# Swapped-query loads of the first four latent-attention units, issued from ScalarE's DMA queue

## The chip, the cores and the metric

The kernel runs on one core of a Trainium2 chip. The metric is the time of one execution on the device, in microseconds (us). The engines have short names in the rows of the profile: PE is TensorE (matmuls; PEld is its weight loads), DVE is VectorE, ACT is ScalarE, POOL is GpSimd, SP is SyncE. Each works through its own list of instructions in order. A data transfer (DMA) is an instruction too: an engine issues it, and it then runs beside the engines. "SPq" in a row is SyncE issuing DMAs.

## The reference, cut to what matters

Two layers of a decoder trunk, sequence length 1024, width 1024, everything in float32. Each layer projects its input, runs four token mixers (latent attention with a rotary key, stick-breaking attention, forgetting attention, memory attention), gates and merges them, projects the merge and normalises. The change touches the latent attention (MLA):

```python
q = (_rms_norm(c_q, q_norm) @ w_qb).reshape(b, s, 4, 64 + 32)
q_nope, q_pe = q[..., :64], q[..., 64:]
q_pe = _rope(q_pe, cos[:, :, None, :], sin[:, :, None, :])
kv = (_rms_norm(c_kv, kv_norm) @ w_kvb).reshape(b, s, 4, 64 + 64)
k_nope, v_mla = kv[..., :64], kv[..., 64:]
k_pe = jnp.broadcast_to(_rope(k_rope[:, :, None, :], ...), (b, s, 4, 32))
y_mla = _causal_softmax_attention(concat([q_nope, q_pe], -1), concat([k_nope, k_pe], -1), v_mla)
...
merged = sum over the four mixers n of merge_g[n] * ((branch[n] * silu(gate_z[n])) @ w_branch[n])
x = layer_norm(alpha * x + merged @ w_out)
```

## The kernel before

TensorE multiplies in a reduced float32 format, so each value is split into a high and a low part, and a product is made of passes over such parts (L257 to L259 for the projections). For the attention the two parts of a head's query lie above each other in one operand: 64 rows high, 64 rows low. `stack_pair` writes these operands from a projection, `opA` for one head and `opB` for the next: the high parts by ACT (L310), the low parts by DVE (L314). Each holds 512 queries, a "half" of the sequence.

A unit of attention is one head with 256 queries (`qg` is 0 to 3; half = `qg // 2`), and `run` goes through the units in a list. A unit's scores are made per 128 queries in pieces of up to 512 keys, each piece by three matmuls into one tile `sc`: L385 (query operand by keys), L386 (the same slice of the query operand with its high and low rows exchanged, by the same keys), and L388 (rotary part `qpe` by `kpe`). DVE then takes the masked scores' maximum (L443), ACT the exponential (L135), POOL scales (L455), TensorE transposes (L474), and the values follow (L504).

The exchanged slice is `s2` (tile name `s` in the rows), and `swapped` makes it: it takes one of three buffers and copies the two 64-row halves crosswise with two DMAs of 64 KB, L365 and L366. `Unit.prep` calls it, and `run` calls `prep` one unit ahead. A scheduler then orders each engine's instructions from the order in which they are written, so that a DMA stands in its engine's list at about the place where its operand is ready.

The latent attention comes last in a layer. Ahead of it a chain of steps makes its operands: `mla_qpe(half)` projects the rotary queries, rotates them on DVE (L1059 to L1063), splits them (`CAST qrs`, L1065, on ACT for the high part; L1066 on POOL for the low part), stores both parts with four DMAs to a scratch array `qr_d` in device memory (L1069) and loads them back in another layout as four `qpe` tiles (L1074). `mla_q(half)` projects the queries and makes `opA` and `opB`. The order is `mla_qpe(1)`, `mla_q(1)`, `mla_qpe(0)`, `mla_q(0)`. The first two units of the list use half 1, the third and the fourth half 0. Between these steps, and then between the pieces of the units, stands work of `merge`: its matmuls `pg` and `pb`, `tanh` on ACT (`mg`, L135), an accumulation on DVE (`acc`, L1122), and loads of the other mixers' results (`y`, L1086, four at a time, split later at L158 and L159).

All of these DMAs are issued by SyncE, in order. Each raises one of eight counters (`DMAHW0` to `DMAHW7`), which are given out in turn, and a DMA that is given a counter waits until the DMA that had the counter before it has landed; it does so on the engine that issues it, in order.

Of the kernel before, what the change touches and what calls it, by code (L numbers as in the profile page):

```python
# [66 lines left out]
def decoder_trunk(ctx: ExitStack, tc: tile.TileContext, x, x_t, mem_t, positions, w_a, w_s, mla_q_norm, mla_w_qb,  # L67
                  mla_kv_norm, mla_w_kvb, fox_forget_bias, w_out,
                  ln_gain, ln_bias, out, dump=None):
    nc = tc.nc  # L70
    act, dve, pool, pe = nc.scalar, nc.vector, nc.gpsimd, nc.tensor
# [15 lines left out]
    def nm(s):  # L87
        uid[0] += 1
        return f"{s}_{uid[0]}"
# [33 lines left out]
    def f(ap):  # L123
        return ap.bitcast(F32)
# [139 lines left out]
    class Stream:  # L264


        def __init__(self):
            self.next = 0
            self.blocks = []
# [89 lines left out]
        yield  # L359


    def swapped(q, head, qg):
        s2 = tp.tile([P, 256], F32R, tag="s2", name=nm("s2"), bufs=3)
        src = q[head][qg // 2][:, (qg % 2) * 256:(qg % 2) * 256 + 256]
        nc.sync.dma_start(f(s2[0:64, :]), f(src[64:128, :]))  # L365
        nc.sync.dma_start(f(s2[64:128, :]), f(src[0:64, :]))  # L366
        return s2

    class Unit:


        def __init__(self, op, head, qg, kind, aux=None):
            self.op, self.head, self.qg, self.kind, self.aux = op, head, qg, kind, aux
            self.p = []

        def prep(self):
            self.s2 = swapped(self.op["q"], self.head, self.qg)
            if self.kind == "fox":
                self.aux()

# [140 lines left out]
    def drain(g):  # L521
        for _ in g:
            pass

    def steps(g, n):
        for _ in range(n):
            if next(g, 0) == 0:
                return
# [3 lines left out]
    def finish(filler, every, over=lambda: None):  # L532

        while flight:
            for _ in flight.pop(0).values():
                steps(filler, every)
        while products:
            product()
            steps(filler, every)
        over()  # L540
        drain(filler)

    def run(units, filler, total, rest=True):


        order = list(units)
        gaps = sum(len(u.chunks()) * 2 + (1 if u.kind == "mem" else 2 + 2 * (u.qg // 2)) for u in units)
        done = [0, 0]

        def gap():  # L550
            done[0] += 1
            want = done[0] * total // gaps
            steps(filler, want - done[1])
            done[1] = want

        for i, u in enumerate(order):
            if i == 0:
                u.prep()
            if i + 1 < len(order):
                order[i + 1].prep()  # L560
            for _ in u.scores():
                gap()
            flight.append(u)
            if len(flight) > AHEAD:
                for _ in flight.pop(0).values():
                    gap()
        if rest:
            drain(filler)
# [101 lines left out]
    for layer in range(DEPTH):  # L670
# [101 lines left out]
        def units(op, kind):  # L772
            return [Unit(op, h, g, kind) for h in range(2) for g in Q_ORDER]
# [416 lines left out]
        mla = units(ml[0], "mla") + units(ml[1], "mla")  # L1190

        mla[1], mla[2] = mla[2], mla[1]
        run(mla, mg, 96 - MG_EARLY - MG_LATE, False)
        finish(mg, 1, lambda: prep.__setitem__(0, True))
        for pair in range(2):
# [144 lines left out]
```

## Time and profile before

| | |
|---|---|
| time, median of 3 runs | 1580.02 us (1576.14 to 1580.74) |
| the profiled execution | 1578.76 us, of which the span of the trace is 1577.0 |
| TensorE busy | 1549.5 us, 98% of the span, 8382 matmuls |
| VectorE, ScalarE, GpSimd busy | 1033.9, 715.8 and 783.8 us (66, 45 and 50%) |
| DMA | 139.46 MB, 88 GB/s on average |
| swapped queries from `opA` and from `opB` | 128 DMAs each, 64 KB |

A row of the timeline gives the start in us from the begin of the span, the duration, the engine, the line, the operation with what it writes and reads, the shape, and in brackets the idle time of the engine just before it with what ended that. A row of SPq with "x4" is four issues in a row. "PEclk" and "clock" are the share of TensorE's full clock that was granted.

### The profile page before, as it was taken

How to read it: one execution, taken by the hardware profiler on the slowest of the kernel's cores; microseconds unless marked ns; L12 is line 12 of the kernel's file. 1: busy time of each engine (PE TensorE's matmuls, PEld its weight loads, DVE VectorE, ACT ScalarE, POOL GpSimd, SP SyncE). 2: the span in 40 equal slices, each digit the busy share in tenths (PEclk: the TensorE clock that was granted, in tenths of full speed). 3: DMA queues.
4: the chain of work that ended last, by engine and by line, in shares of the span. 5: the costliest groups of instructions: out<-in, count | busy, mean ns of one | idle time of the engine just before them, and what ended most of it. 6: DMA issues, size and time to landing. Idle time of an engine off the chain costs nothing.

```text
span 1577.0 us, 24654 instructions
## 1 busy us (share of the span) xinstructions
PE 1549.5 (98%) x8382; PEld 1325.1 (84%) x8382; DVE 1033.9 (66%) x2031; ACT 715.8 (45%) x1582; POOL 783.8 (50%) x955
## 2 busy tenths in 40 slices
PE   9999999999999899999999999999999998999997
PEld 8888888888888688888898888888888887888886
DVE  7455697755437688882853566887554376888738
ACT  4355665545434466440323556655354345664300
POOL 5666545665545333671336655465565443436600
PEclk9999999999999999999999999999999999999999
DMA  6322112242234511252313211122422253212413
GB/s 185 114 71 68 44 44 70 64 121 79 74 109 134 151 39 60 77 162 89 124 57 105 59 50 45 42 73 64 121 78 81 99 159 119 68 39 80 154 51 116
DMA packets 91694, 139.46 MB, mean 88 GB/s; under 512 B 13936, under 2 KB 39344, under 8 KB 91568
## 3 DMA queue, kind: packets, MB, share of 16 engines
q1 hardware_dynamic: 91568, 137.88, 28.7%
q8 instruction: 67, 1.10, 0.3%
q14 instruction: 59, 0.48, 0.1%
HBM read 95.86 MB, written 25.20 MB: 77 GB/s over the span
## 4 chain that ended last, share of the span: by engine, by line
PE 88%; DVE 4%; DMA 2%; POOL 2%; issue 2%; ACT 1%; SPq 0%; DVEq 0%; ACTq 0%; POOLq 0%
PE pj L257 13%; PE pj L259 13%; PE pj L258 13%; PE y L504 7%; PE pt L474 6%; PE po L258 4%; PE po L257 4%; PE po L259 4%; PE sc L386 4%; PE sc L385 3%; PE pb L257 3%; PE pb L258 2%; PE pb L259 2%; DMA s<-opA 1%; PE pg L257 1%
## 5 line engine op out<-in xcount | busy, mean ns | idle before, releaser
L257 PE MATMUL pj<-xTh,wh 128*128 128x512 f32 x832 | 334.6, 402 | 2.3 <-DVE mx L443 1.4
L259 PE MATMUL pj<-xTh,wl 128*128 128x512 f32 x832 | 327.5, 394 | 0.0
L258 PE MATMUL pj<-xTl,wh 128*128 128x512 f32 x832 | 326.4, 392 | 0.0
L167 POOL TENSOR_TENSOR wl<-wr,wh 128x512 fp32r<-128x512 f32 x168 | 223.9, 1335 | 10.4 <-PE pj L259 0.8
L156 DVE TENSOR_TENSOR pl<-pt,ph 128x512 fp32r<-128x512 f32 (+1 forms) x272 | 171.5, 638 | 87.8 <-ACT ph L155 85.5
L164 POOL TENSOR_SCALAR wh<-wr 128x512 fp32r<-128x512 f32 x168 | 114.1, 680 | 205.4 <-PE pj L258 145.8
L155 ACT CAST ph<-pt 128x512 fp32r<-128x512 f32 (+1 forms) x272 | 147.2, 549 | 150.6 <-PE pt L474 145.9
L455 POOL TENSOR_SCALAR p<-p,sm 128x896 f32<-128x896 f32 (+7 forms) x128 | 102.9, 805 | 181.0 <-DVE sm L454 140.0
L259 PEld LDWEIGHTS pj<-xTh,wl 128*128 128x128 f32 x832 | 156.3, 188 | 31.6
L257 PEld LDWEIGHTS pj<-xTh,wh 128*128 128x128 f32 x832 | 156.7, 188 | 25.0 <-DVE mx L443 1.8
L258 PEld LDWEIGHTS pj<-xTl,wh 128*128 128x128 f32 x832 | 156.7, 188 | 22.7
L135 ACT ACTIVATE p<-p,mx 128x896 f32<-128x896 f32 (+7 forms) x128 | 99.5, 777 | 84.8 <-DVE mx L443 73.4
L504 PE MATMUL y<-pl,v 128*128 128x256 f32 (+1 forms) x544 | 121.9, 303 | 0.0
L135 ACT ACTIVATE mg<-pg 128x512 f32<-128x512 f32 x128 | 75.8, 597 | 97.5 <-PE pg L259 53.6
L504 PE MATMUL y<-ph,v 128*128 128x256 f32 (+1 forms) x544 | 111.1, 280 | 0.1
L474 PE MATMUL pt<-ident_r,p 128*128 128x128 f32 x704 | 110.8, 273 | 0.2
L448 DVE TENSOR_TENSOR_SCAN kt<-kt,unseen 128x896 f32<-128x896 f32 (+3 forms) x64 | 96.0, 1503 | 19.8 <-ACT kt L135 19.3
L504 PEld LDWEIGHTS y<-ph,v 128*128 128x128 f32 x544 | 94.8, 189 | 14.1 <-issue 0.9
L257 PE MATMUL pb<-ybh,wh 128*128 128x512 f32 x256 | 101.9, 398 | 3.3 <-DVE mgl L156 1.9
L258 PE MATMUL pb<-ybl,wh 128*128 128x512 f32 x256 | 100.1, 391 | 0.0
L259 PE MATMUL pb<-ybh,wl 128*128 128x512 f32 x256 | 100.1, 391 | 0.0
L474 PEld LDWEIGHTS pt<-ident_r,p 128*128 128x128 f32 x704 | 84.7, 140 | 13.9 <-DVE pl L156 0.7
(270 smaller groups left out, 3529.0 us busy)
## 6 DMA issues: line engine op xcount, KB each, us to landing
wr<-in_w_s_dram SPq DMA_DIRECT2D x168, 256.0 KB
s<-opA SPq DMA_DIRECT2D x128, 64.0 KB
s<-opB SPq DMA_DIRECT2D x128, 64.0 KB
wr<-in_w_out_dram SPq DMA_DIRECT2D x32, 256.0 KB
xr<-in_x_t_dram SPq DMA_DIRECT2D x16, 256.0 KB
ckb<-c_d SPq DMA_DIRECT2D x8, 512.0 KB
y_d<-y SPq DMA_DIRECT2D x16, 256.0 KB
qr_d<-qrs SPq DMA_DIRECT2D x16, 256.0 KB
```

The source lines that it names most:

```text
L135: i = act.activation(*args, **kw)
L155: act.copy(h, src)
L156: return dve.tensor_tensor(l, src, f(h), ALU.subtract)
L164: i = pool.tensor_scalar(h, src, 1.0, 1.0, ALU.mult, ALU.mult)
L167: pool.tensor_tensor(l, src, f(h), ALU.subtract)
L257: pe.matmul(ps, ah, bh, start=k == 0, stop=False)
L258: pe.matmul(ps, ah, bl, start=False, stop=False)
L259: pe.matmul(ps, al, bh, start=False, stop=k == nk - 1)
L448: dve.tensor_tensor_scan(kt[:, ::-1], kt[:, ::-1], unseen[:, S - w:][:, ::-1], 1.0, ALU.mult, ALU.max)
L455: pool.tensor_scalar(p, p, sm, 1.0, ALU.mult, ALU.mult)
L474: pe.transpose(pt[:, c:c + P], self.p[i][:, b * P:(b + 1) * P], ident)
L504: pe.matmul(u.y[:, q0 * P:256], u.op["v"][b][:, u.head, :], src[:, s * 256 + q0 * P:s * 256 + 256], start=j == 0 and n == 0, stop=j == n_c ...
```

## The change

`swapped` takes the queue as an argument, a unit has SyncE's queue by default, and the first four units of the latent attention get ScalarE's.

```diff
-    def swapped(q, head, qg):
+    def swapped(q, head, qg, queue):
         s2 = tp.tile([P, 256], F32R, tag="s2", name=nm("s2"), bufs=3)
         src = q[head][qg // 2][:, (qg % 2) * 256:(qg % 2) * 256 + 256]
-        nc.sync.dma_start(f(s2[0:64, :]), f(src[64:128, :]))
-        nc.sync.dma_start(f(s2[64:128, :]), f(src[0:64, :]))
+        queue.dma_start(f(s2[0:64, :]), f(src[64:128, :]))
+        queue.dma_start(f(s2[64:128, :]), f(src[0:64, :]))
         return s2
...
             self.op, self.head, self.qg, self.kind, self.aux = op, head, qg, kind, aux
             self.p = []
+            self.queue = nc.sync
 
         def prep(self):
-            self.s2 = swapped(self.op["q"], self.head, self.qg)
+            self.s2 = swapped(self.op["q"], self.head, self.qg, self.queue)
...
         mla[1], mla[2] = mla[2], mla[1]
+        for u in mla[:4]:
+            u.queue = act
         run(mla, mg, 96 - MG_EARLY - MG_LATE, False)
```

Four units, two halves and two layers make 16 DMAs that leave SP's list and stand in ACT's. The order of PE, DVE and POOL is the same. Because of the added lines, a line below the edit has a number up to 3 higher after it (L1074 is L1075, L1065 is L1066). In the rows below a wait names the engine or the DMA counter that the instruction waits for; the numbers behind the names of tiles tell buffers apart.

ACT in layer 0, around the split of half 0's rotary queries (`qrs`); `s_1446` and `s_1447` are the first and second unit's swapped queries. Before:

```order
L135 ACTIVATE mg_6113<-pg_6109 128x512 [waits DVE_49,Activation_49]
L310 ACTIVATE opA_6082<-pj_6063 64x512 [waits PE_49]
L310 ACTIVATE opB_6083<-pj_6063 64x512 [waits DMAHW0_49]
L135 ACTIVATE mg_6135<-pg_6131 128x512 [waits DVE_49,PE_49,Activation_49]
L1065 CAST qrs_6147<-qr_6118 128x512 [waits DVE_49]
```

ACT at the same place after the change:

```order
L135 ACTIVATE mg_6113<-pg_6109 128x512 [waits DVE_49,Activation_49]
L366 DMA s_1446_6215<-opA_6057 64x256 [waits DMAHW0_49,Activation_49]
L310 ACTIVATE opA_6082<-pj_6063 64x512 [waits PE_49]
L310 ACTIVATE opB_6083<-pj_6063 64x512
L135 ACTIVATE mg_6135<-pg_6131 128x512 [waits DVE_49,PE_49]
L365 DMA s_1446_6215<-opA_6057 64x256 [waits DMAHW4_49,DVE_49]
L365 DMA s_1447_6218<-opA_6057 64x256 [waits DMAHW6_49,DMAHW3_49]
L366 DMA s_1447_6218<-opA_6057 64x256 [waits DMAHW0_49]
L1066 CAST qrs_6147<-qr_6118 128x512 [waits DVE_49]
```

Three of the four DMAs stand directly ahead of the split. `DMAHW4` and `DMAHW6` are there the first and the third `qpe` load of half 1, `DMAHW0` is the first unit's own first half. In layer 1 the same DMAs stand at the same place one counter on: they wait for the second and the fourth `qpe` load and for the first `y` load.

ACT in layer 0, around the first unit's first exponential (`p_6221`); `s_1460` and `s_1475` belong to the third and the fourth unit. Before:

```order
L310 ACTIVATE opB_6210<-pj_6190 64x512
L135 ACTIVATE p_6221,sm_6223<-p_6221,mx_6222 128x896 [waits DVE_49]
L135 ACTIVATE mg_6248<-pg_6244 128x512 [waits PE_49,Activation_49]
L135 ACTIVATE p_6237,sm_6239<-p_6237,mx_6238 128x1024 [waits DVE_49]
L135 ACTIVATE p_6262,sm_6264<-p_6262,mx_6263 128x640 [waits DVE_49,Pool_49]
```

And after:

```order
L310 ACTIVATE opB_6210<-pj_6190 64x512
L366 DMA s_1460_6259<-opA_6184 64x256 [waits DMAHW2_49,Activation_49]
L135 ACTIVATE p_6221,sm_6223<-p_6221,mx_6222 128x896 [waits DVE_49]
L365 DMA s_1460_6259<-opA_6184 64x256 [waits DMAHW3_49,DVE_49]
L135 ACTIVATE mg_6248<-pg_6244 128x512 [waits PE_49]
L365 DMA s_1475_6309<-opA_6184 64x256 [waits DMAHW4_49,PE_49]
L366 DMA s_1475_6309<-opA_6184 64x256 [waits DMAHW5_49]
L135 ACTIVATE p_6237,sm_6239<-p_6237,mx_6238 128x1024 [waits DVE_49]
```

`DMAHW2` to `DMAHW5` are here the four stores of `qr_d` of half 0. The exponential stands behind a DMA that waits for the first of them, the `tanh` behind one that waits for the second. In layer 1 the third unit's first DMA stands behind the first exponential.

SP in layer 0, from the last `qpe` load of half 1 to the first store of half 0. Before:

```order
L1074 DMA qpe_5989<-qr_d 128x1x512 [waits DMAHW7_49,PE_49]
L366 DMA s_1446_6215<-opA_6057 64x256 [waits Activation_49]
L1086 DMA y_6095<-y_d 128x512 [waits DVE_49,PE_49]
L1086 DMA y_6097<-y_d 128x512 [waits DVE_49]
L1086 DMA y_6099<-y_d 128x512 [waits DVE_49]
L1086 DMA y_6101<-y_d 128x512 [waits DMAHW4_49,DVE_49]
L365 DMA s_1446_6215<-opA_6057 64x256 [waits DMAHW5_49,DVE_49]
L365 DMA s_1447_6218<-opA_6057 64x256 [waits DMAHW6_49]
L366 DMA s_1447_6218<-opA_6057 64x256 [waits DMAHW7_49]
L233 DMA wr_6663<-in_w_s_dram 128x512 [waits DMAHW0_49,Pool_49]
L789 DMA gq_9509<-in_mla_q_norm_dram 128x3x1 [waits DMAHW1_49]
L1069 DMA qr_d<-qrs_6147 128x512 [waits DMAHW2_49,Activation_49]
```

And after:

```order
L1075 DMA qpe_5989<-qr_d 128x1x512 [waits DMAHW7_49,PE_49]
L790 DMA gq_9509<-in_mla_q_norm_dram 128x3x1 [waits DVE_49]
L1087 DMA y_6095<-y_d 128x512 [waits PE_49]
L1087 DMA y_6097<-y_d 128x512
L1087 DMA y_6099<-y_d 128x512 [waits DMAHW5_49]
L1087 DMA y_6101<-y_d 128x512 [waits DMAHW7_49]
L233 DMA wr_6663<-in_w_s_dram 128x512 [waits DMAHW1_49,Pool_49]
L1070 DMA qr_d<-qrs_6147 128x512 [waits DMAHW2_49,Activation_49]
```

The four swapped-query DMAs are gone from between the `qpe` loads and the stores, the small load `gq` stands ahead of the `y` loads, and the third and the fourth `y` load wait for the second and the fourth `qpe` load.

## The prediction

> **What bounds the kernel now.** I read the page first, then TensorE's waits, then the timelines of TensorE (PE), SyncE's queue (SPq), ScalarE (ACT) and VectorE (DVE) around the two starts of the latent attention.
>
> ```profile
> span 1577.0 us, 24654 instructions
> PE 1549.5 (98%) x8382; PEld 1325.1 (84%) x8382; DVE 1033.9 (66%) x2031; ACT 715.8 (45%) x1582; POOL 783.8 (50%) x955
> ```
> TensorE is the bound; only what keeps it idle or slow can be won. Its waits, longest first (us in total, times, longest):
>
> ```profile
> PE sc L386 <- DMA s<-opA: 5.5, 3, 2.5
> PE sc L386 <- DMA wr<-in_w_s_dram: 3.4, 1, 3.4
> ```
> L386 multiplies with the swapped queries (`s2`, shown as `s`). The second row has the wrong name: that instruction waits only for the two halves of `s2`. PE in layer 0, then in layer 1 (start, duration; idle before it):
>
> ```profile
> 521.30 0.39 PE L385 MATMUL sc<-opA,opA 128*128 128x512 f32 x1
> 525.06 0.47 PE L386 MATMUL sc<-opA,s 128*128 128x512 f32 x1 [3.37 <-DMA wr<-in_w_s_dram]
> 526.56 0.69 PE L385 MATMUL sc<-opA,opA 128*128 128x384 f32 x1 [0.79 <-DVE mx L443]
> 530.45 0.39 PE L386 MATMUL sc<-opA,s 128*128 128x512 f32 x1
> 530.68 0.40 PE L388 MATMUL sc<-kpe,qpe 128*128 128x512 f32 x1
> 537.98 0.30 PE L386 MATMUL sc<-opA,s 128*128 128x128 f32 x1 [2.46 <-DMA s<-opA]
> 545.62 0.50 PE L257 MATMUL pb<-ybh,wh 128*128 128x512 f32 x1 [0.56 <-DVE acc L1122]
> ...
> 1305.08 0.39 PE L385 MATMUL sc<-opA,opA 128*128 128x512 f32 x1
> 1307.91 0.71 PE L386 MATMUL sc<-opA,s 128*128 128x512 f32 x1 [2.44 <-DMA s<-opA]
> 1309.84 0.69 PE L385 MATMUL sc<-opA,opA 128*128 128x384 f32 x1 [0.79 <-DVE mx L443]
> 1311.88 0.79 PE L385 MATMUL sc<-opA,opA 128*128 128x512 f32 x1 [0.72 <-DVE mx L443]
> 1320.60 0.30 PE L386 MATMUL sc<-opA,s 128*128 128x128 f32 x1 [0.60 <-DMA s<-opA]
> ```
> The first unit waits 3.37 and 2.44 us, the third 2.46 and 0.60. Behind each first wait the clock falls (columns: PE, PEld, DVE, ACT, POOL busy, clock, DMA share, GB/s), and DVE fills up:
>
> ```profile
> 526.00:530.00 4.00, 3.44 (x9) 2.75 (x9) 3.11 (x7) 1.14 (x2) 0.00 (x0) 0.57 0.39 149
> 528.00:536.00 8.00, 7.51 (x33) 5.62 (x32) 7.63 (x22) 4.26 (x8) 3.46 (x4) 0.89 0.46 143
> 1308.00:1315.00 7.00, 5.49 (x13) 3.64 (x14) 4.37 (x10) 1.23 (x3) 0.00 (x0) 0.51 0.44 161
> 1311.20:1317.20 6.00, 5.32 (x17) 4.31 (x18) 5.78 (x13) 1.88 (x4) 0.86 (x1) 0.70 0.42 137
> ```
> Why `s2` is late: SPq issues it behind the `qpe` and `y` loads.
>
> ```profile
> 511.55 2.74 SPq L1074 DMA_DIRECT2D qpe<-qr_d  x4
> 514.94 1.98 SPq L1086 DMA_DIRECT2D y<-y_d  x4
> 517.22 2.36 SPq L365 DMA_DIRECT2D s<-opA  x2
> 521.36 0.46 SPq L366 DMA_DIRECT2D s<-opA  x1
> 523.35 2.24 SPq L1069 DMA_DIRECT2D qr_d<-qrs  x4
> 528.57 2.61 SPq L1074 DMA_DIRECT2D qpe<-qr_d  x4
> ...
> 1289.06 2.19 SPq L1069 DMA_DIRECT2D qr_d<-qrs  x4
> 1293.21 2.66 SPq L1074 DMA_DIRECT2D qpe<-qr_d  x4
> 1299.27 2.99 SPq L365 DMA_DIRECT2D s<-opA  x2
> 1304.13 0.46 SPq L366 DMA_DIRECT2D s<-opA  x1
> 1305.54 2.70 SPq L1069 DMA_DIRECT2D qr_d<-qrs  x4
> ```
>
> **The new loads, first unit.** Sixteen issues move to ACT. ACT issued none before; by SPq's rows one takes 0.46 to 0.6 us, so about 4.2 us a layer, in an engine 45% busy. Layer 0: the first half leaves before CAST, the second after the first `qpe` load has landed. SPq's last `y` issue had that same wait and ended at 516.92, so it left by 516.4, and so can the half on ACT. How long until it lands is not shown for ACT's queue. Long end: 517.22 to 525.06, 7.8 us, behind everything on SPq. Short end: 1291.25 (the last store's issue done) to 1293.21 (all four landed), 2.0 us. I take 2.5, nearer to the short end, since ACT's own queue holds nothing else. PE needs it at 521.53, so up to 5.1 would do: the 3.37 goes. In layer 1 the second half waits for the second `qpe` load and leaves at 1299.3, as on SPq; 2.5 us later is ahead of 1305.31: the 2.44 goes.
>
> [...]
>
> **What DVE makes of it.** ACT and POOL rows, then DVE rows, layer 0 ahead of layer 1:
>
> ```profile
> 516.26 0.62 ACT L1065 CAST qrs<-qr 128x512 fp32r<-128x512 f32 x1 [4.92 <-DVE qr L1063]
> 528.59 1.05 ACT L135 ACTIVATE p<-p,mx 128x896 f32<-128x896 f32 x1 [6.33 <-DVE mx L443]
> 1300.04 0.62 ACT L1065 CAST qrs<-qr 128x512 fp32r<-128x512 f32 x1 [4.92 <-DVE qr L1063]
> 1300.74 1.29 POOL L1066 TENSOR_TENSOR qrs<-qr,qrs 128x512 fp32r<-128x512 f32 x1 [4.51 <-ACT qrs L1065]
> 1305.45 0.59 ACT L310 ACTIVATE opB<-pj 64x512 fp32r<-64x512 f32 x1
> ...
> 525.80 0.69 DVE L443 CUSTOM_DVE_ANT_0 p<-sc,mask 128x512 f32<-128x512 f32 x1 [5.96 <-PE sc L388]
> 527.93 0.62 DVE L443 CUSTOM_DVE_ANT_0 p<-sc,mask,mx 128x384 f32<-128x384 f32 x1 [0.82 <-PE sc L388]
> 1309.08 0.69 DVE L443 CUSTOM_DVE_ANT_0 p<-sc,mask 128x512 f32<-128x512 f32 x1 [5.40 <-PE sc L388]
> 1311.20 0.62 DVE L443 CUSTOM_DVE_ANT_0 p<-sc,mask,mx 128x384 f32<-128x384 f32 x1 [1.42 <-PE sc L388]
> ```
> Matmuls at full clock follow each other by 0.23 (530.45 to 530.68). Layer 0: L386 starts at 521.53 instead of 525.06; the first maximum follows 0.7 later, at 522.2 (was 525.80). PE's second piece follows that by 0.76 as before, 522.95 (was 526.56): the 0.79 stays. Its second maximum came 1.37 later at about half clock; at full clock, with three passes 0.14 shorter each, 0.95: 523.9, 4.0 earlier than 527.93. Layer 1 by the same steps: L386 at 1305.31, first maximum 1306.0, second piece 1306.7, second maximum 1307.7, 3.5 earlier than 1311.20. From there DVE is 95% busy (7.63 of 8, 5.78 of 6), so it passes on 4.0 and 3.5 and no more, however fast PE is.
>
> **The third unit.** Layer 0: its first half on ACT waits for the first `qr_d` store. SPq now sends the fourth `y` load only after the fourth `qpe` load has landed (by 521.36), then a weight load and the stores: first one at about 522.5, 0.8 earlier than 523.35. The four landed by 528.57, 5.2 after the first issue, the first about three issues sooner, 3.3. So ACT issues the half at 525.8, does the exp (528.59 before) at 526.4, and the other half at 527.5; `s2` is there at 530.5. Without waits PE would want it at 531.4 (535.5 less 4.0). The half-0 `qpe` loads leave at 527.7; the first such load took at most 4.9 (511.55 to 516.4), so 4.5, 532.2. The unit starts about 532.3 instead of 537.98. But the next work there hangs on ACT and DVE, which used that gap: the acc at 545.62 needs tanh and copies which stand behind the moved exps. I take 4.5 gained there: 4.0 and a quarter of the 2.46. Layer 1: the 0.60 goes, and I keep 3.7 of 3.5 to 4.1.
>
> **What the moved waits hold up.** Layer 1: the second unit's halves wait for the fourth `qpe` load (landed by 1304.13) and the first `y` load (about 1304.8, since the stores behind it leave at 1305.54), so CAST goes from 1300.04 to 1305.4. Behind it stand POOL's other half of `qrs` (1.29 us, begun 0.08 behind CAST), which the third and fourth store carry: they leave at 1307.4 and 1308.0, where before the last of the four left at 1307.6, so `qpe` slips 0.4; and the four copies that ended at 1306.04 and now end near 1308.9. DVE wants the second copy after its second maximum and one acc, at 1309.0; it is done at 1307.8 (a tanh and two copies of 0.6 each behind CAST's end at 1306.0). The cover is 1.2 us; each us beyond it costs one. Layer 0: CAST at about 519.8, after the third `qpe` load (landed 519.1, when the second of the `s` issues of 517.22 left); copies end 522.8, no one waits. SPq loses 16 issues. Its third and fourth `y` loads now wait there for the second and fourth `qpe` load, so the fourth leaves at 521.4 instead of 516.4; it is split only after the third unit has started (537.98 before, 532.3 now), ten us on, which covers it. POOL's order is the same.
>
> **Sum.** -4.5 and -3.7: 8.2 us. The profiled execution took 1578.76 (span 1577.0 and 1.8 around it): 1570.6. The median of the runs, 1580.02, lies 1.3 above it; I say 1571. The ends: the first waits alone, without any gain in pace, 3.37 + 2.44 = 5.8; everything, 3.37 + 0.79 + 2.46 + 2.44 + 0.79 + 0.72 + 0.60 = 11.2, plus the slow clock, (1 - 0.57) x 4 + (1 - 0.51) x 7 = 5.1: 16.3, 1562.5.
>
> **Rivals.** *All of it (10%)*: DVE is no bound because the order relaxes: 1562 to 1566. Against it: 95% busy.
>
> *No new road (20%)*: the backlog lies in the shared engines, not in SPq's queue. Then layer 1's half, issued at the same 1299.3, lands no sooner: 0 there. Layer 0's has only two `y` loads ahead instead of four and lands between 521.4 and 525.1, say 523.2: 1.9 won; with the third unit's earlier issue 3.5 in all, 1575.3. For it: 7.8 us for 64 KB shows a real backlog. [...]
>
> *ACT held up, slower (8%)*: ACT works in order, so the exp waits for the first store, the tanh behind it for the second. It decides if the first store lands after 528.0 (528.59 less an issue), 2.2 later than I take: then the exp is later than before. At 530 every piece behind is 2 later in each layer, the first waits' gain gone: 1583. Against it: those stores had landed by 528.57 in a fuller queue.
>
> The forecast keeps 62%. About 0.3%, 4.7 us, is what a measurement tells from no change. Faster 0.68: nine tenths of the forecast (0.56), all of it (0.10), a tenth of no new road (0.02). Same 0.24: the rest of these two. Slower 0.08. Range 1564 to 1578; the forecast's own is 1567 to 1574.
>
> **What would show it.** Right: no L386 wait near 521.5 and 1305.3, clock 1.0 in both stages, CAST 3 to 5 us later and the exp still earlier, DVE without gaps after the second maximum. Wrong: L386 still waiting with `s2` issued early (shared backlog), or PE waiting on ACT's tanh or DVE's `opB` copy (ACT held up).

## The result and the profile after

The changed kernel takes 1568.60 us (median of 4 runs, 1567.52 to 1569.40) against 1579.26 us before (4 runs, 1576.14 to 1580.74). The ratio is 0.9935, with a 95% interval of 0.9917 to 0.9952: 10.7 us less. The forecast was 1571 us, with 8.2 us less.

The page of the kernel after, its busy times, and then TensorE's rows in the list of waits (us in total, times, longest):

```profile
PE 1545.6 (99%) x8382; PEld 1321.3 (84%) x8382; DVE 1038.9 (66%) x2031; ACT 715.6 (46%) x1582; POOL 783.9 (50%) x955
...
PE sc L386 <- DVE mx L444: 2.3, 3, 0.8
PE sc L386 <- DVE opB L314: 1.0, 2, 0.6
PE sc L387 <- DMA s<-opA: 0.8, 2, 0.4
```

The two rows on swapped queries, 5.5 and 3.4 us before, have become one of 0.8. The waits on the maximum stay at 2.3, and one on DVE's low part of `opB` is new (1.0). (L386, L387 and L389 are now the three score matmuls.) PE's timeline after, at the two starts of the latent attention, layer 0 and layer 1:

```profile
521.84 0.39 PE L386 MATMUL sc<-opA,opA 128*128 128x512 f32 x1
522.64 0.47 PE L387 MATMUL sc<-opA,s 128*128 128x512 f32 x1 [0.42 <-DMA s<-opA]
524.13 0.45 PE L386 MATMUL sc<-opA,opA 128*128 128x384 f32 x1 [0.79 <-DVE mx L444]
527.19 0.47 PE L386 MATMUL sc<-opA,opA 128*128 128x512 f32 x1 [0.56 <-DVE opB L314]
532.42 0.28 PE L387 MATMUL sc<-opA,s 128*128 128x128 f32 x1
540.40 0.50 PE L257 MATMUL pb<-ybh,wh 128*128 128x512 f32 x1 [0.86 <-DVE acc L1123]
...
1298.99 0.39 PE L386 MATMUL sc<-opA,opA 128*128 128x512 f32 x1
1299.79 0.50 PE L387 MATMUL sc<-opA,s 128*128 128x512 f32 x1 [0.41 <-DMA s<-opA]
1304.95 0.47 PE L386 MATMUL sc<-opA,opA 128*128 128x512 f32 x1 [0.47 <-DVE opB L314]
1318.17 0.50 PE L257 MATMUL pb<-ybh,wh 128*128 128x512 f32 x1 [0.85 <-DVE acc L1123]
```

The `pb` that waits for `acc` in layer 1, before (its fellow in layer 0, 545.62, is in the prediction):

```profile
1328.21 0.50 PE L257 MATMUL pb<-ybh,wh 128*128 128x512 f32 x1 [0.57 <-DVE acc L1122]
```

From the first unit's first matmul to this `pb`, layer 0 took 545.62 less 521.30, 24.32 us, and now takes 540.40 less 521.84, 18.56: 5.76 less. Layer 1 went from 1328.21 less 1305.08, 23.13, to 1318.17 less 1298.99, 19.18: 3.95 less. Together that is 9.71 of the 11.2 us by which the span fell (1577.0 to 1565.8). Outside these two stretches the first one begins 0.54 later, and the stretches between them and behind them are 0.87 and 1.16 shorter. Two later waits of the merge (`pb` for DVE's `mgl`) go with that: they were 0.73 and 1.22 and are now none and 0.43, together 1.52. They vary from kernel to kernel in no clear relation to the gain: in the single traces of the ten kernels below the first lies between none and 0.79, the second between none and 1.23.

The third unit's halves in SP's queue before, behind the four `qpe` loads of 528.57:

```profile
531.23 0.51 SPq L366 DMA_DIRECT2D s<-opA  x1
531.79 1.23 SPq L365 DMA_DIRECT2D s<-opA  x2
```

The queues after (ACTq is ScalarE issuing DMAs; "x2" is two issues, and the time between them is counted in), then the rows of ACT and DVE that the forecast spoke of:

```profile
514.84 6.67 SPq L1087 DMA_DIRECT2D y<-y_d  x4
528.06 2.52 SPq L1075 DMA_DIRECT2D qpe<-qr_d  x4
1287.64 2.67 SPq L1075 DMA_DIRECT2D qpe<-qr_d  x4
...
515.56 3.77 ACTq L365 DMA_DIRECT2D s<-opA  x2
526.14 0.47 ACTq L366 DMA_DIRECT2D s<-opA  x1
526.76 0.50 ACTq L365 DMA_DIRECT2D s<-opA  x1
1293.01 5.15 ACTq L365 DMA_DIRECT2D s<-opA  x2
...
520.02 0.62 ACT L1066 CAST qrs<-qr 128x512 fp32r<-128x512 f32 x1 [8.16 <-DVE acc L1123]
526.65 1.04 ACT L135 ACTIVATE p<-p,mx 128x896 f32<-128x896 f32 x1 [3.18 <-DVE opA L314]
1298.85 0.62 ACT L1066 CAST qrs<-qr 128x512 fp32r<-128x512 f32 x1 [9.84 <-DMA y<-y_d]
...
524.98 0.62 DVE L444 CUSTOM_DVE_ANT_0 p<-sc,mask,mx 128x384 f32<-128x384 f32 x1 [0.30 <-PE sc L389]
1302.14 0.62 DVE L444 CUSTOM_DVE_ANT_0 p<-sc,mask,mx 128x384 f32<-128x384 f32 x1 [0.90 <-PE sc L389]
```

What to see here: the first unit's second half was issued at 515.56 and PE could use it at 522.64, 7.1 us later; in layer 1 at 1293.01 and 1299.79, 6.8 us. So on ACT's queue, with nothing else ahead of it there, the load was 0.8 and 1.8 us quicker than on SP's (7.8 before, and 1299.27 to 1307.91, 8.6), and still took some 7. The third unit's halves leave ACT at 526.14 and 526.76, ahead of the four `qpe` loads of 528.06. And the split (CAST), ahead of which ACT does no work for 8.16 us (4.92 before), comes at 520.02, with the exponential still 1.9 us earlier than before (526.65, was 528.59).

Windows of after, by engine (columns as in the prediction), at the places that were slow before, and then while the first unit's second half is under way, layer 0 and layer 1:

```profile
526.00:530.00 4.00, 3.44 (x15) 2.50 (x14) 3.81 (x8) 1.74 (x3) 0.49 (x1) 1.00 0.57 171
525.00:533.00 8.00, 7.44 (x38) 5.65 (x37) 7.63 (x23) 4.21 (x8) 3.41 (x4) 1.00 0.60 204
1303.00:1311.00 8.00, 7.53 (x39) 6.02 (x40) 7.63 (x23) 4.25 (x9) 3.64 (x4) 1.00 0.47 155
515.56:522.64 7.08, 6.67 (x30) 5.22 (x29) 2.45 (x4) 2.57 (x5) 1.29 (x1) 1.00 0.85 225
1293.01:1299.79 6.78, 6.37 (x30) 4.93 (x28) 2.16 (x4) 0.94 (x2) 0.24 (x1) 1.00 0.98 240
```

The clock is 1.00 throughout (0.57 before in the first window), DVE is busy for 7.63 us of 8 in both layers, and the DMA engines are 0.85 and 0.98 busy while the half is under way.

### The profile page after: what moved, and what is told of

It reads as the page before. It is cut to its first block, busy times and chain, and to the rows that moved or that the text cites. A ratio compares the mean times of both kernels' runs of the same rounds, so it can differ in the third digit from the quotient of the medians.

```text
span 1565.8 us, 24652 instructions
## 1 busy us (share of the span) xinstructions
PE 1545.6 (99%) x8382; PEld 1321.3 (84%) x8382; DVE 1038.9 (66%) x2031; ACT 715.6 (46%) x1582; POOL 783.9 (50%) x955
## 4 chain that ended last, share of the span: by engine, by line
PE 95%; DVE 2%; DMA 2%; ACT 1%; issue 0%; SPq 0%; POOL 0%; DVEq 0%; ACTq 0%
PE pj L257 13%; PE pj L259 13%; PE pj L258 13%; PE y L505 8%; PE pt L475 7%; PE po L259 4%; PE po L257 4%; PE po L258 4%; PE sc L387 4%; PE sc L386 4%; PE pb L257 4%; PE pb L258 3%; PE pb L259 3%; PE pg L257 2%; PE pg L258 2%; PE pg L259 2%
```

## The experiments

Ten kernels, each with a change against the kernel before or after. The ratio is to the kernel before in the same comparison, where that took 1578.30 to 1579.26 us. The waits are PE's idle time ahead of the first and of the third unit's first matmul with swapped queries, layer 0 / layer 1, in us, from one trace of each kernel.

| kernel | time | ratio to before, 95% | first unit | third unit |
|---|---|---|---|---|
| before | 1579.26 | | 3.37 / 2.44 | 2.46 / 0.60 |
| after | 1568.60 | 0.9917 to 0.9952 | 0.42 / 0.41 | none |
| e1: first two units on ACT | 1579.63 | 0.9994 to 1.0014 | 0.92 / none | 5.81 / 3.60 |
| e2: third and fourth on ACT | 1573.85 | 0.9963 to 0.9994 | 2.77 / 1.35 | none |
| e3: `qpe` rows at one stride, SP | 1564.49 | 0.9894 to 0.9924 | 0.52 / none | none |
| e4: the same, with the change | 1564.76 | 0.9893 to 0.9923 | none | none |
| e5: `y` later, SP | 1583.57 | 1.0016 to 1.0038 | 1.00 / none | 5.50 / 4.34 |
| e6: `y` later, with the change | 1578.11 | 0.9979 to 1.0000 | none | 1.32 / none |
| e7: `y` on ACT, queries on SP | 1578.85 | 0.9989 to 1.0008 | none | 5.38 / none |
| e9: `qpe` behind third unit, SP | 1569.45 | 0.9924 to 0.9953 | 3.72 / 1.25 | none |
| e10: e3 and e9 together | 1562.94 | 0.9887 to 0.9920 | none / 0.19 | none |
| e11: e1 and e9 together | 1567.16 | 0.9917 to 0.9947 | 1.46 / none | none |

### Which of the four units earns it: e1 and e2

```diff
-        for u in mla[:4]:
+        for u in mla[:2]:      # e1
+        for u in mla[2:4]:     # e2
```

> Only the first two units' swapped queries on ACT; the third and fourth unit's stay on SP. My theory (each unit's loads win their own wait): the first waits shrink as after the whole change (0.4 us each), but the third unit's wait comes back, since PE reaches it about 3 us sooner and SP issues its halves behind the four qpe loads of half 0: 1 to 2.5 us of wait in layer 0, 0.6 to 2 in layer 1. Total gain 5 to 7.5 us instead of 10.7: 1572 to 1574. Rival (the third and fourth unit's loads earn nothing, the first wait is all): 1568 to 1570.

> Only the third and fourth unit's loads on ACT. My theory: the first waits stay at 3.4 and 2.4 us with the slow clock behind them; the third unit's waits of 2.46 and 0.60 go to below 0.3; gain 2 to 3 us: 1576 to 1577.5. Rival (ACT is held up by the waits for the stores, which land later here than after the whole change): the first exponential starts later than 528.6, no gain or a loss: 1579 to 1582.

Measured: e1 1579.63 us, no gain at all; e2 1573.85 us, 4.9 us less by the medians and 3.3 by the ratio (1 to 6 by its interval). The traced execution of e1 took 1583.22, the longest of its ten, so its waits may be longer than usual. PE in e1, layer 0 (two rows) and layer 1, with the first of the third unit's two issues on SP in layer 0:

```profile
524.04 0.47 PE L387 MATMUL sc<-opA,s 128*128 128x512 f32 x1 [0.92 <-DMA s<-opA]
540.23 0.45 PE L387 MATMUL sc<-opA,s 128*128 128x128 f32 x1 [5.81 <-DMA s<-opA]
1324.04 0.30 PE L387 MATMUL sc<-opA,s 128*128 128x128 f32 x1 [3.60 <-DMA s<-opA]
...
532.28 0.52 SPq L366 DMA_DIRECT2D s<-opA  x1
```

The first waits shrink as after the whole change, and all of it is lost again at the third unit, whose wait grows by 3.35 and 3.00: its halves stand in SP's queue behind half 0's `qpe` loads until 532.28, and PE can use them only 8 us after that. I had expected the loss to be 1 to 2.5 us. The result misses both theories: a shorter first wait alone is worth nothing as long as the third unit's is there to take it back. In e2 it is the other way round, the first waits stay and the third unit's go (layer 0):

```profile
524.40 0.77 PE L387 MATMUL sc<-opA,s 128*128 128x512 f32 x1 [2.77 <-DMA wr<-in_w_s_dram]
```

The third unit's waits were 3.06 us in all, and the first waits are 0.60 and 1.09 shorter too; the interval does not settle whether the gain is more than 3.06. The first exponential comes at 528.41 (528.59 before), so the wait for the first store did not hold it up; the second one stands 2.10 us behind ACT's own DMA, without a loss in the total.

### What makes the loads late: e3, e4, e5

The eight-engine theory needs a word. The source of a `qpe` load is 8 groups of 16 rows (shape 8 x 16 x 512). In the kernel before, in the 1.2 us from 514.20 on, by SP's issues almost only `qpe` loads are under way (the next issues left at 514.33 and 514.94, and the first `qpe` issue, of 511.55, had moved nothing before 513.00). The 16 DMA engines are 0.53 busy there, at 205 GB/s:

```profile
514.20:515.40 1.20, 1.20 (x7) 0.98 (x6) 1.19 (x2) 0.00 (x0) 0.00 (x0) 1.00 0.53 205
```

0.53 of 16 is 8.5: that about eight of them carry these loads is an estimate from this share. e3 changes the rows' order in memory from (t, head, c) to (t, c, head), so that a head's 128 rows lie at one stride, and leaves all queues alone.

```diff
-            src = f(qr_d[half]).rearrange("r a (t h c) n -> h (r a t) c n", t=2, h=4)
+            src = f(qr_d[half]).rearrange("r a (t c h) n -> h (r a t c) n", t=2, h=4)
# and the same order of rows in the projection's weights (load_wq) and in the rotary tables
# e4: this and the change
# e5, against before:
-                if ct == KT - (3 if first else 2) and following is not None:
+                if ct == KT - 2 and following is not None:
                     load_y(following)
```

> All swapped queries stay on SP; the rotary queries lie in another row order, so that each qpe load is 128 rows at one stride and runs on 16 DMA engines instead of 8. Theory A (the swapped queries are late because the eight engines that carry the qpe loads are backed up): the four qpe loads land in about 5 us instead of 9.6, the first waits of 3.4 and 2.4 us fall below 1, gain 6 to 9 us, 1570 to 1573, without any second queue. Theory B (they are late because they stand behind qpe and y in SP's own order, 2 MB in all): the bytes ahead are the same and the wait stays above 2 us in layer 0: gain under 3 us, 1576 to 1580.

> All swapped queries stay on SP; the four y loads are written one block of the merge later, so that in SP's list they stand behind the qpe loads of half 0 and no longer ahead of the swapped queries. Theory B (y ahead of them in SP's order makes them late): issued near 515, landed by 521, first waits below 1 us in both layers, gain 5 to 8 us, 1571 to 1574. Theory A (the qpe loads on eight engines make them late): they still land behind the qpe loads, near 521 to 523, the first wait in layer 0 keeps 1 to 2 us, gain 2 to 4 us. In both the y loads may now hold up the third unit's halves, which stand behind them.

> The whole change and, beside it, the qpe loads on 16 engines. Theory A (the change is a way round the eight backed-up engines, and of no use once they are not backed up): 1563 to 1567, the same as the qpe loads on 16 engines alone (1564.5). Rival 1 (a queue of its own is worth something by itself): the first wait in layer 0, 0.52 us there, goes, and so do further waits: below 1563. Rival 2 (the waits on ACT cost, hidden so far behind the gain): above 1567.

Measured: e3 1564.49 us, 14.3 below before and some 4 below the change (their intervals overlap a little), with nothing on ACT. SP in e3, from the first `qpe` issue to the second unit's second half, and PE's first wait there:

```profile
510.37 1.75 SPq L1075 DMA_DIRECT2D qpe<-qr_d  x4
514.81 1.11 SPq L365 DMA_DIRECT2D s<-opA  x2
516.04 0.51 SPq L366 DMA_DIRECT2D s<-opA  x1
...
521.37 0.48 PE L386 MATMUL sc<-opA,s 128*128 128x512 f32 x1 [0.52 <-DMA wr<-in_w_s_dram]
```

Two us of the stretch in which the `qpe` loads move, from 1.2 us behind their first issue on, in the kernel before and then in e3 (the last two columns are the DMA engines' mean busy share and GB/s):

```profile
512.80:514.80 2.00, 2.00 (x11) 1.65 (x10) 1.98 (x3) 0.00 (x0) 0.00 (x0) 1.00 0.39 104
```

```profile
511.60:513.60 2.00, 2.00 (x10) 1.66 (x9) 1.97 (x4) 0.00 (x0) 0.02 (x1) 1.00 0.96 299
```

And the kernel before while the first unit's second half is under way:

```profile
517.22:525.06 7.84, 4.47 (x20) 3.41 (x19) 1.28 (x2) 2.85 (x5) 1.03 (x1) 1.00 0.94 256
```

SP issues the same DMAs in the same order, and the second unit's second half leaves only when the fourth `qpe` load has landed. That was at most 9.8 us behind the first `qpe` issue before (521.36 less 511.55) and is at most 5.7 in e3 (516.04 less 510.37). The engines are 0.96 instead of 0.39 busy while the `qpe` loads move, and 0.96 of 16 is 15.4. (Which engines these are, no row here shows: that the row order makes the loads late is measured, that it does so by the number of engines is an estimate from these shares.) So in the kernel before the engines are little used at first and full later, 0.94, when the first unit's second half is under way. The half's own way is not much shorter in e3: 6.6 us from its issue to its use (514.81 to 521.37), 7.8 before. Of the 2.85 us that the first wait lost, 1.3 come from this, 1.2 from the half leaving sooner behind the first `qpe` issue, and 0.3 from PE arriving later. The forecast of theory A (1570 to 1573) was too careful, since the third unit's waits go too. With e3 in place, the change adds nothing: e4 is 1564.76, the same, although the first unit no longer waits at all. So in this kernel the change is a way round that backlog and has no worth of its own; nor do its waits on ACT cost anything that can be measured there.

e5 shows that the `y` loads count as well. Without them ahead the first wait falls from 3.37 to 1.00 and from 2.44 to none, as theory B has it and nearly as far as in e3. Here too the half still takes 7.1 us (issue at 515.58, use at 522.64); most of what it wins is that it leaves 1.7 us sooner behind the first `qpe` issue. But the kernel is 4.8 us slower, since the `y` loads now stand ahead of the third unit's halves (layer 0):

```profile
522.64 0.48 PE L386 MATMUL sc<-opA,s 128*128 128x512 f32 x1 [1.00 <-DMA s<-opA]
540.58 0.45 PE L386 MATMUL sc<-opA,s 128*128 128x128 f32 x1 [5.50 <-DMA s<-opA]
```

I had named that danger and given it no number. So either load out of the way takes most of the first wait, and neither theory alone explains it; of these two only e3 takes the third unit's waits too.

### Queue or order: e9, e6 and e7

```diff
# e9, against before: half 0's qpe loads are issued by the third unit's prep, behind its swapped queries
+        mla[2].then = lambda: load_qpe(0)
# e6: the change, and y later as in e5
# e7, against before: only the y loads that feed merge(1) go to ACT
-                        nc.sync.dma_start(y, y_d[r:r + P, half * HALF:(half + 1) * HALF])
+                        (act if n == 1 else nc.sync).dma_start(y, ...)
```

> All swapped queries on SP; half 0's qpe loads are written behind the third unit's swapped queries, so that SP issues those first. The third unit's gain is then had without a second queue, if it comes from the order alone: its waits of 2.46 and 0.60 fall below 0.5, as with the third and fourth unit's loads on ACT (1573.9), unless the qpe loads, now later, hold up L388 of the third unit by about 1 us: 1573 to 1577. Rival (it needs ACT's queue): its wait stays above 2 us, no gain: 1578 to 1581.

> The whole change with the y loads behind half 0's qpe loads, to be compared with the same y loads and all swapped queries on SP (1583.6, first wait 1.00, third unit's waits 5.5 and 4.3 us). If ACT's queue is a road of its own, the first unit's second half lands 2 to 3 us after its issue and the first wait is gone; if the eight engines are shared, it still lands near 522 and the first wait stays near 1 us. In both the third unit's halves, now issued on ACT ahead of the qpe and y loads, are in time, and their waits go: 1570 to 1575.

> All swapped queries on SP; the four y loads are issued from ACT instead, so that on SP only the qpe loads stand ahead of the first unit's second half. If the order in SP's queue is what counts, the first wait falls to 1 us or less in both layers; if the bytes in the shared engines count, it stays above 2. The third unit's halves stay behind half 0's qpe loads, and PE comes sooner: their waits grow to 4 to 6 and 3 to 4 us, so that little is won in all: 1576 to 1582.

Measured: e9 1569.45 us, 3.5 below the lower end that I expected and as good as the change, with one queue. It keeps first waits of 3.72 (shown) and 1.25; its third unit does not wait:

```profile
525.14 0.77 PE L389 MATMUL sc<-opA,s 128*128 128x512 f32 x1 [3.72 <-DMA wr<-in_w_s_dram]
```

So with the `qpe` loads as they are, the third unit needs its loads ahead of them, on whichever queue; in e3, with the other row order, its loads stand behind the `qpe` loads and it does not wait. That e9 gains more than e2 goes with the scheduler's other order of the first pieces: PE's waits of 0.79 and 0.72 us for the maximum are not in its trace. No run tests this by itself.

e6 and e7 show the price of DMAs in ACT's list. ACT and PE in e6, layer 0, and PE in layer 1:

```profile
529.16 2.74 ACTq L365 DMA_DIRECT2D s<-opA  x2
533.67 0.47 ACTq L366 DMA_DIRECT2D s<-opA  x1
534.19 1.15 ACT L135 ACTIVATE p<-p,mx 128x1024 f32<-128x1024 f32 x1 [5.39 <-DMA s<-opA]
...
536.16 0.30 PE L387 MATMUL sc<-opA,s 128*128 128x128 f32 x1 [1.32 <-DMA s<-opA]
1317.76 0.80 PE L257 MATMUL pg<-mrh,wh 128*128 128x512 f32 x1 [3.15 <-DVE acc L1123]
```

ACT sits idle for 5.39 us behind its own DMA, and the second exponential comes at 534.19 instead of 530.23 in the trace of after. In layer 1 the same exponential stands 4.16 us behind ACT's DMA; on DVE an `acc` stands behind work that needs this exponential, and PE waits 3.15 us for that `acc`. The first wait is gone as expected of a road of its own, but that load was also issued some 4 us earlier than in e5, so e6 cannot tell the two apart. The total, 1578.11, misses the 1570 to 1575. ACT and PE in e7, layer 1:

```profile
1294.94 8.23 ACTq L1086 DMA_DIRECT2D y<-y_d  x2
...
1303.86 0.72 PE L257 MATMUL pg<-mrh,wh 128*128 128x512 f32 x1 [3.38 <-ACT mg L135]
```

The third and fourth `y` issue keep ACT until 1303.2; the `tanh` behind them is late and PE waits 3.38 us for it. This is the rival *ACT held up*, in another place than I had put it. In e7 the first waits are gone, as expected if the order in SP's queue counts, but this does not decide against the engines: PE comes to the first unit 1.1 and 5.3 us later behind the first `qpe` issue than before, and in layer 0 the half leaves 1.1 us sooner. The third unit's wait grew to 5.38 in layer 0, as expected; in layer 1, where I had expected 3 to 4, there is none.

### Putting the parts together: e10 and e11

> Nothing on ACT: the qpe loads on 16 engines (alone 1564.5) and half 0's qpe loads behind the third unit's swapped queries (alone 1569.5). If both cure the same backlog, together they give little more than the first alone, whose third unit no longer waits: 1562 to 1565. If the second also saves DVE's waits at the start of the units by its other order (0.79 and 0.72 us were gone with it), 1560 to 1562. If the later qpe loads now hold up the third unit: above 1566.

> The first two units' swapped queries on ACT (alone no gain, because the third unit's waits grew to 5.8 and 3.6 us) and half 0's qpe loads on SP behind the third unit's swapped queries (alone 1569.5, first waits 3.7 and 1.3 us left). My theory, two separate places: the first waits fall to 0.4 to 0.9 and the third unit does not wait; the gains of the two parts add to 9.7 and 3 to 4 us: 1565 to 1568. Rival (there is one sum of work for the eight engines and what the first units win the third always loses): 1570 or more.

Measured: e10 1562.94 us, the fastest of all, 15.4 us below the kernel before in its own comparison and some 5 below the change by the ratios; its interval overlaps that of e3 (1564.49), so the second part's own worth there is not settled. e11, 1567.16, is in the expected range: the first waits' gain, lost in e1, is partly kept once the third unit is provided for. In e10 PE waits for a DMA only once in the two starts, 0.19 us. PE in e11, layer 0 and then layer 1:

```profile
522.81 0.47 PE L390 MATMUL sc<-opA,s 128*128 128x512 f32 x1 [1.46 <-DMA s<-opA]
538.00 0.41 PE L390 MATMUL sc<-opA,s 128*128 128x384 f32 x1 [0.81 <-DMA s<-opA]
1301.58 0.41 PE L389 MATMUL sc<-opA,opA 128*128 128x384 f32 x1 [1.41 <-DVE opB L314]
```

The 0.81 is the fourth unit's, whose halves are still behind the `qpe` loads. The 1.41 is ACT held up once more: DVE's copies wait 2.08 us there for ACT's copy of `opB`, which comes behind the split and the DMAs ahead of it.

## Why the prediction was right, step by step

The time, 1568.60, lies in the range and in the forecast's own range, on the side of more gain. The trace shows which terms carried it.

**The new loads, first unit: the term that was wrong.** I let a load on ACT land 2.5 us after its issue, between 2.0 and 7.8, "since ACT's own queue holds nothing else". It took 7.1 and 6.8 us until PE could start: next to the long end. The wait still fell to 0.42, because the issue was at 515.56, 0.8 earlier than the 516.4 that I had read off the last `y` issue, because PE wanted the half only at 522.22, 0.7 later than the 521.53 of the forecast, and because up to 5.1 us were to spare. In layer 1 I let it leave as on SPq, 6.1 us behind the first `qpe` issue; it left 5.4 behind (1293.01 less 1287.64), and the 2.44 fell to 0.41. That the error does not show in the time is luck: with 7.1 and 6.8 in place of 2.5 my own sum leaves waits of 2.0 and 0.8 (516.4 + 7.1 against 521.53, 1299.3 + 6.8 against 1305.31). On the road, then, the rival *no new road* was nearer: a second queue gave 0.8 and 1.8 us, and while the load was under way the DMA engines were 0.85 and 0.98 busy. Even the 0.8 is not the queue's alone: two of the four `y` loads left behind this load, not ahead of it. On the time it was wrong, since it gave the first waits only 1.9 and 0, where 2.95 and 2.03 came. That a 64 KB load on an empty queue passes the others was my estimate; no run shows it, and the trace of after speaks against it at both places, with 7.1 and 6.8 us.

**What DVE makes of it: right, a little large.** From the unit's first matmul to the second maximum: 527.93 less 521.30, 6.63, became 524.98 less 521.84, 3.14: 3.5 earlier, forecast 4.0. Layer 1: 1311.20 less 1305.08, 6.12, became 3.15: 3.0, forecast 3.5. The remaining waits of 0.42 and 0.41 are nearly all of the difference. The 0.79 stayed, the clock was 1.00 and DVE was full, as said.

**The third unit: right in place, too small in size.** Forecast start 532.3, measured 532.42 without a wait. The first store was there when the exponential needed it (issue at 526.14, forecast 525.8; exponential at 526.65, forecast 526.4). But I kept only a quarter of the 2.46 because the `acc` behind it was to be late. Its wait grew from 0.56 to 0.86, by 0.30, not by 1.8. So 5.76 us were won in layer 0 where 4.5 were forecast, and 3.95 in layer 1 where 3.7 were. This is most of the difference on the stage, 9.71 against 8.2. What I missed altogether is how much hangs on this unit: e1 shows that without its part the change would have given nothing.

**What the moved waits hold up: right.** CAST came at 520.02 (forecast 519.8); in layer 1 it moved from 6.8 us behind the first `qpe` issue (1300.04 less 1293.21) to 11.2 (1298.85 less 1287.64), 4.4 later where I had 5.4. The fourth `y` load left at about 521.0 to 521.5 (forecast 521.4). The copies behind CAST end later, and PE has a new wait for `opB` of 0.56 and 0.47 us. But that is DVE's own low part: ACT's last copies had ended at 523.47 and 1302.29, and e3, with nothing on ACT, has waits for `opB` of 0.56 and 0.47 us as well. It is the full DVE that is late, not ACT. *ACT held up* did not happen here; e6 and e7, and e11 in one place, show that it does when ACT's waits come later or its copies are needed sooner.

**Outside the sum:** the two later waits of the merge, 1.52 us between the two traces, were in none of my terms. Since they come and go in the other kernels too, whatever these gain, I do not count them as the change's; no run was made for them, and their cause is open.

## What to carry to other kernels

When a load is late, ask what is ahead of it in the DMA engines before asking which queue issues it: here one change of row order, with which four 256 KB loads kept the engines 0.96 instead of 0.39 busy, was worth 14.3 us where the second queue gave 10.7, and made the second queue useless (1564.76 us with it, 1564.49 without). Follow a wait that you remove to the next instruction that wants the same resource, since e1 won 2.4 us in each layer and lost 3 or more at the next use of the queue, some 15 us later. A DMA in a compute engine's list brought its waits along, and they cost where the transfer waited for was late: in layer 1 of e6 ACT stood idle for 4.16 us behind its DMA, and PE then waited 3.15 us.

## What the runs showed of the hardware

A 64 KB load issued on a queue that held nothing else ahead of it still took 6.8 to 7.1 us until TensorE could use it, while other loads kept the engines 0.85 and 0.98 busy (the last two windows of after). Loads of the same size were issued and moved faster with 128 rows at one stride than with 8 groups of 16 rows: the same four issues took 1.75 instead of 2.74 us (the first rows of SPq in e3 and in the prediction), and in two us in which they moved the engines' share rose from 0.39 to 0.96 and the rate from 104 to 299 GB/s (the windows of 512.80 in the kernel before and of 511.60 in e3).
